# Decoder trunk on one core: M and VO stored in DRAM as high and low parts, a few multiplications and squares on ScalarE, weight sums spread anew

## The chip, the cores and the metric

One Trainium2 chip, one of its cores. The metric is the device time of one launch in microseconds, the median of several runs. The kernel before takes 3073.2 us (three runs, 3071.1 to 3073.73).

## What is computed

One inference step of a hybrid decoder trunk (one layer, width 1024) for a prompt of 2048 tokens and 8 sample tokens, all in float32. Cut to what matters here:

```
h = rmsnorm(x, g_mix);  z = h @ w_in -> u | q | k | v
group A: causal pooling of u;  group B: differential attention, 4 heads:
    w = softmax(q0 k0) - lam * softmax(q1 k1);  o = rmsnorm(w @ v, subln_g) * (1 - lam_0)
x = x + concat(pool, o) @ w_out
cross attention, 4 heads, 256 memory tokens:
    q = rmsnorm(x, g_cross) @ wq;  a = softmax(q @ mem_k / 16);  x = x + (a @ mem_v) @ wo
gated MLP with a causal convolution:  up = rmsnorm(x, g_ffn) @ w_up;  x = x + (silu(g) * a) @ w_down
y = rmsnorm(x, g_final)
```

## The kernel before

The prompt is worked through in four chunks (c = 0 to 3) of 512 tokens; the 8 sample tokens ride with chunk 3. A float32 product is made from three matmuls (`mm3`, lines 97 to 101): each operand is split into a high part in the PE's float32r format and the low rest, and high x low, high x high and low x high are added up. `split` (lines 92 to 95) makes the parts: ScalarE (ACT) casts the high part, VectorE (DVE) subtracts it.

Cross attention is folded: for each head h, M = wq_h mem_k_h^T and VO = mem_v_h wo_h are computed once (`m_head`, `vo_head`, lines 536 to 576), so that the scores of a chunk are h2 @ M and the result is A @ VO. Both are evacuated from PSUM in pieces of 128x512 by a copy on ACT (lines 557 and 573, 16 each) and stored in DRAM (`m_d`, `vo_d`) from ACT's queue; each chunk loads them again: 8 tiles of M (two for a head) in `scores`, 8 tiles of VO (one for each 128 output columns) in `vo`.

Every weight tile goes through the class `Weight` (lines 297 to 313) in three stages: 0 loads the raw tile on SyncE's queue (SP), 1 casts the high part on ACT (line 307), 2 subtracts the low part on DVE (line 310). `drive` takes the items of the program in order and calls the stages ahead of use: `look(4, 3, 2)` means that the raw load is called four tiles ahead, the cast three, the subtraction two.

```python
        if n == 0:
            self.raw = H("wraw")
            SY.dma_start(v3(self.raw, self.k), self.src)
        elif n == 1 and not self.only_raw:
            self.hi = H("whi", F32R)
            S.copy(self.hi[:, :1024], self.raw[:, :1024])
        elif n == 2 and not self.only_raw:
            self.lo = H("wlo", F32R)
            V.tensor_tensor(self.lo[:, :1024], self.raw[:, :1024], f(self.hi[:, :1024]), ALU.subtract)
```

All large tiles come from one ring of 41 buffers (`H`), the tiles of 512 columns from one ring of 6 (`St`), the small ones from a ring of 16; a new tile waits until the one that had its buffer is released. PSUM has two double banks (`PA`) and four single ones (`PB`). Each engine executes its own instructions in a fixed order, which the framework's scheduler sets from the program's items; no time in this text comes from it.

The items of the stages are woven into each other by `weave` at the end of the function: main work (PE) and extra work (norms, loads, the sample group) by their costs. Among the extras are the weight sums (`sums_items`, lines 1534 to 1573): the MLP's up-projection is done with seven products in place of eight, and needs sums of blocks of `w_up`. For each of 22 column blocks j there are two quarters q, and a quarter takes four loads of 128 KB, four DVE instructions of 256 columns (lines 1552 to 1555), one split of 128x1024 and two stores of 512 KB from POOL's queue. They are spread over four stretches of the program: the input projection of chunks 0 and 1, the attention of chunks 0 and 1, the attention of chunks 2 and 3, and the cross attention of chunks 2 and 3 right ahead of the MLP.

Other lines that the change touches: `k_evac` (line 743, a cast of the keys on DVE), `att_post1` (lines 1198 to 1211, the norm after attention: squares on ACT at 1201, their sums on DVE at 1203, the scaling on DVE at 1210), and `softmax` in `scores` (line 1306, the division of the exponentials on DVE; ACT makes the exponentials at 1304).

## Time and profile before

| what | value |
|---|---|
| median of three runs | 3073.2 us |
| the profiled execution's own time | 3072.26 us |
| its span | 3070.5 us |
| PE busy | 2934.5 us, 96% of the span |
| PE weight loads busy (beside PE) | 2644.1 us, 86% |
| DVE busy | 2243.7 us, 73% |
| ACT busy | 1353.3 us, 44% |
| POOL busy | 459.7 us, 15% |
| DMA, mean | 222 GB/s |
| mean granted PE clock | 0.982 |

The trace of this execution is read by stretch. From the start to about 115 us lie M and VO of heads 0 and 1 with the first norms; to 295 us the input projection; to 650 us the attention of chunks 0 and 1 with the projections of chunks 2 and 3; to 1057 us the attention of chunks 2 and 3, with M and VO of heads 2 and 3 and the scores of chunk 0 woven in; to 1540 us the rest of cross attention; then the MLP, with VO of chunk 3 inside its first 90 us. A matmul on this page counts as busy also while it waits in the pipeline, so the stretches are compared by idle time and by what ended it, not by the busy share.

### The profile page before, as it was taken

The page shows a single profiled execution, that of the slowest core. Times are in us where ns is not written, and L with a number is a line of the kernel's source. Part 1 is how long each engine was busy: PE and PEld are TensorE (multiplying, and loading weights), DVE is VectorE, ACT ScalarE, POOL GpSimd, SP SyncE. Part 2 cuts the span into 40 slices and gives each one's busy share as a digit, 9 for nine tenths or more (in the row PEclk, how much of TensorE's full clock was granted, in tenths as well). Part 3 has the DMA queues.
Part 4 walks back from the last instruction along what each step waited for, and adds up shares of the span by engine and source line. Part 5 has one row for each costly group of instructions (what it writes and reads, how often), then busy time and mean ns, then how long its engine had stood idle before and what let it go on. Part 6 is the DMA issues. An engine that isn't in the chain of part 4 may idle for free.

```text
span 3070.5 us, 52699 instructions
## 1 busy us (share of the span) xinstructions
PE 2934.5 (96%) x19806; PEld 2644.1 (86%) x19806; DVE 2243.7 (73%) x4168; ACT 1353.3 (44%) x2271; POOL 459.7 (15%) x865
## 2 busy tenths in 40 slices
PE   7999999999999889899999999999999999999998
PEld 6789889978888779598888899888898989899998
DVE  5745777667767577667768978888788777877777
ACT  4544455455656424343443344434444433443333
POOL 0244224200000041611100000010000010000000
PEclk9999999999999999999999999999999999999999
DMA  8797578654554467668579876777767686576762
GB/s 277 231 299 244 168 248 272 203 181 143 163 165 128 132 201 235 191 222 307 191 229 337 279 258 192 262 244 243 248 226 259 218 277 211 173 268 221 242 207 103
DMA packets 522627, 683.17 MB, mean 222 GB/s; under 512 B 29585, under 2 KB 344472, under 8 KB 522356
## 3 DMA queue, kind: packets, MB, share of 16 engines
q1 hardware_dynamic: 468637, 533.88, 53.9%
q0 software_dynamic: 39936, 135.17, 12.6%
q10 hardware_dynamic: 13798, 10.76, 1.1%
q8 instruction: 156, 2.56, 0.3%
q14 instruction: 100, 0.81, 0.1%
HBM read 549.12 MB, written 130.98 MB: 221 GB/s over the span
## 4 chain that ended last, share of the span: by engine, by line
PE 60%; DVE 6%; DMA 3%; issue 2%; ACT 2%; POOL 1%; SPq 0%; DVEq 0%; ACTq 0%; POOLq 0%
PE up L1640 15%; PE down L1756 15%; PE up L1642 7%; PE wo L487 4%; PE upB L1640 2%; PE S L99 2%; PE S L100 2%; PE S L101 2%; PE O L1175 1%; PE upB L1642 1%; PE vo L101 1%; PE vo L99 1%; PE vo L100 1%; DMA vg<-in_cache_v_dram,idx 1%; PE sc L1122 1%
## 5 line engine op out<-in xcount | busy, mean ns | idle before, releaser
L1756 PE MATMUL down<-act,whi 128*128 128x512 f32 (+1 forms) x1760 | 450.0, 350 | 0.2 <-DVE xf L1760 0.2
L1640 PE MATMUL up<-xhi,shl 128*128 128x256 f32 (+1 forms) x2816 | 405.5, 285 | 8.7 <-DVE s L1645 4.6
L1640 PEld LDWEIGHTS up<-xhi,shl 128*128 128x128 f32 x2816 | 365.5, 188 | 37.5 <-ACT s L1655 14.3
L1694 ACT ACTIVATE cc<-Uf,vec 128x512 f32<-128x512 f32 (+1 forms) x176 | 144.0, 818 | 494.7 <-DVE Uf L1645 476.9
L310 DVE TENSOR_TENSOR wlo<-wraw,whi 128x1024 fp32r<-128x1024 f32 x256 | 309.8, 1218 | 42.4 <-ACT whi L307 35.7
L1756 PEld LDWEIGHTS down<-act,whi 128*128 128x128 f32 x1760 | 285.5, 188 | 32.7 <-DVE xf L1760 1.5
L307 ACT CAST whi<-wraw 128x1024 fp32r<-128x1024 f32 x256 | 265.6, 1046 | 81.7 <-DMA wraw<-in_w_down_dram 22.6
L1756 PE MATMUL down<-act,wlo 128*128 128x512 f32 (+1 forms) x880 | 279.9, 350 | 1.9 <-DVE wlo L310 1.9
L1699 POOL COPY halo<-Uf 128x2 f32<-128x2 f32 x176 | 60.1, 342 | 1321.9 <-DVE Uf L1645 1300.2
L1642 PE MATMUL up<-xlo,shl 128*128 128x256 f32 (+1 forms) x1408 | 223.7, 281 | 0.0
L1140 ACT ACTIVATE T<-T,mn 128x1024 f32<-128x1024 f32 (+4 forms) x192 | 172.0, 897 | 103.2 <-DVE mn L1133 102.4
L1640 PE MATMUL up<-xhi,whl 128*128 128x256 f32 (+1 forms) x1408 | 199.4, 284 | 6.1 <-DVE whl L329 4.6
L1122 PE MATMUL sc<-K,Q 128*128 128x512 f32 (+5 forms) x640 | 172.5, 388 | 25.3 <-DVE mn L1133 25.1
L1640 PEld LDWEIGHTS up<-xhi,whl 128*128 128x128 f32 x1408 | 184.1, 189 | 14.6 <-DVE whl L329 5.8
L1642 PEld LDWEIGHTS up<-xlo,shl 128*128 128x128 f32 x1408 | 191.1, 188 | 0.3
L1702 DVE SCALAR_TENSOR_TENSOR cc<-Uf,vec,cc 128x512 f32<-128x512 f32 x176 | 131.5, 747 | 73.8 <-ACT cc L1694 70.2
L329 DVE TENSOR_TENSOR whl<-wraw,whl 128x512 fp32r<-128x512 f32 x264 | 178.0, 682 | 1.5 <-ACT whl L327 1.5
L1756 PEld LDWEIGHTS down<-act,wlo 128*128 128x128 f32 x880 | 153.7, 188 | 24.8 <-DVE wlo L310 3.5
L1760 DVE TENSOR_TENSOR xf<-xf,down 128x512 f32<-128x512 f32 (+1 forms) x240 | 134.8, 577 | 55.1 <-PE down L1756 53.9
L1645 DVE TENSOR_TENSOR Uf<-up,s 128x256 f32<-128x256 f32 (+1 forms) x264 | 111.4, 422 | 81.2 <-PE up L1642 78.9
L327 ACT CAST whl<-wraw 128x512 fp32r<-128x512 f32 x264 | 154.9, 615 | 30.4 <-PE up L1642 14.8
L1133 DVE CUSTOM_DVE_ANT_0 T<-sc,Dt 128x1024 f32<-128x1024 f32 (+7 forms) x128 | 125.8, 985 | 44.4 <-PE sc L1122 40.5
(434 smaller groups left out, 7068.1 us busy)
## 6 DMA issues: line engine op xcount, KB each, us to landing
shl<-s_d SPq DMA_DIRECT2D x352, 512.0 KB
wraw<-in_w_up_dram SPq DMA_DIRECT2D x264, 256.0 KB
wraw<-in_w_down_dram SPq DMA_DIRECT2D x88, 512.0 KB
ws<-in_w_up_dram SPq DMA_DIRECT2D x176, 128.0 KB
s_d<-shi POOLq DMA_DIRECT2D x44, 512.0 KB, 4.7
s_d<-slo POOLq DMA_DIRECT2D x44, 512.0 KB, 6.7
wraw<-in_w_in_dram SPq DMA_DIRECT2D x32, 512.0 KB
Q<-q_d SPq DMA_DIRECT2D x64, 256.0 KB
```

The lines of the kernel that those rows point to most:

```text
L307: S.copy(self.hi[:, :1024], self.raw[:, :1024])
L310: V.tensor_tensor(self.lo[:, :1024], self.raw[:, :1024], f(self.hi[:, :1024]), ALU.subtract)
L327: S.copy(self.hl[:, :512], self.raw)
L329: V.tensor_tensor(self.hl[:, 512:1024], self.raw, f(self.hl[:, :512]), ALU.subtract)
L1122: PE.matmul(ps[:, j * 512:j * 512 + w], v3(Q[c], 2)[:, z, self.t * P:(self.t + 1) * P], K[c][hf][:, c0:c0 + w], start=z == 0, stop=z == 1)
L1140: S.activation(tg[:, :mg], tg[:, :mg], AF.Exp, bias=mn[:, last:last + 1], scale=-1.0, accum_out=self.l[:, 2 * g + c:2 * g + c + 1])
L1640: PE.matmul(out, wi[:, k, :], xh[:, k], start=k == 0 and wi is wl, stop=False)
L1642: PE.matmul(out, wh[:, k, :], xl[:, k], start=False, stop=k == 3)
L1694: S.activation(cc[:, :w], U[:, 2:2 + w], AF.Identity, bias=vc(CB + nt), scale=vc(CWT + 2 * FT + nt))
L1702: V.scalar_tensor_tensor(cc[:, :CH], U[:, 1:1 + CH], vc(CWT + FT + nt), cc[:, :CH], ALU.mult, ALU.add)
L1756: PE.matmul(out, st["w"][0][wi][:, p, n0:n0 + P], act[:, z + c0:z + c0 + n], start=st_ and p == 0, stop=en and p == g - 1)
L1760: V.tensor_tensor(xx[:, c0:c0 + n], xx[:, c0:c0 + n], out, ALU.add)
```

## The change

M and VO are split when they are evacuated, and both parts are stored: per piece of 128x512, ACT casts the high part, DVE subtracts, and ACT's queue issues two stores. The new class `Parts` loads both parts at stage 2 and has no stages 0 and 1, so the 64 casts and 64 subtractions of these tiles go, and each tile has two loads of 512 KB. The cast of the keys goes from DVE to ACT. In `att_post1` the squares are made in four pieces that also give their sums, and the scaling is four ACT instructions. The division of the softmax is four ACT instructions of 256 columns for each head and chunk. The weight sums' blocks are spread 7, 7, 4, 4 over the four stretches; before, 5, 8, 3, 6.

```diff
-    m_d = dr.tile([NH, 2, P, 1024], F32, name="m_d")
-    vo_d = dr.tile([KT, P, 8, P], F32, name="vo_d")
+    m_d = dr.tile([NH, 2, 2, P, 1024], F32, name="m_d")
+    vo_d = dr.tile([2, KT, P, 8, P], F32, name="vo_d")
...
+    class Parts(Weight):
+        def stage(self, n):
+            if n == 2:
+                self.hi, self.lo = H("dhi", F32R), H("dlo", F32R)
+                for t, src in zip((self.hi, self.lo), self.src):
+                    SY.dma_start(f(v3(t, self.k)), src)
...
     def dram_tile(src, k):
-        return lambda: Weight(src, k)
+        return lambda: Parts(src, k)
...
+    def parts_out(ps, dst, k=1):
+        hi, lo = St("ph", F32R), St("pl", F32R)
+        split(hi[:, :512], lo[:, :512], ps)
+        for t, d in zip((hi, lo), dst):
+            S.dma_start(d, f(t[:, :512] if k == 1 else v3(t, k, 512 // k)))
...
-                ms = St("ms")
-                S.copy(ms[:, :512], ps)
-                S.dma_start(m_d[h, d2 // 2, :, (d2 % 2) * 512:(d2 % 2 + 1) * 512], ms[:, :512])
+                parts_out(ps, [m_d[h, d2 // 2, z, :, (d2 % 2) * 512:(d2 % 2 + 1) * 512] for z in range(2)])
...
-                    vs_ = St("vos")
-                    S.copy(vs_[:, :512], ps)
-                    S.dma_start(vo_d[nh * 4:(nh + 1) * 4, :, h * 2 + i, :].rearrange("n p d -> p n d"), v3(vs_, 4, P))
+                    parts_out(ps, [vo_d[z, nh * 4:(nh + 1) * 4, :, h * 2 + i, :].rearrange("n p d -> p n d")
+                                   for z in range(2)], 4)
...
-        V.tensor_copy(kh[:, :CH], kf[:, :CH])
+        S.copy(kh[:, :CH], kf[:, :CH])
...
-        S.activation(sq[:, :512], O, AF.Square)
-        ss = Tn("oss")
-        V.tensor_reduce(ss[:, 0:4].rearrange("p (a o) -> p a o", o=1), v3(sq, 4, P), AX.X, ALU.add)
+        sq, ss = St("osq"), Tn("oss")
+        for t in range(4):
+            S.activation(sq[:, t * P:(t + 1) * P], O[:, t * P:(t + 1) * P], AF.Square, accum_out=ss[:, t:t + 1])
...
-        V.tensor_tensor(v3(on, 4, P), v3(O, 4, P), bc(r, [P, 4, P], 2), ALU.mult)
+        for t in range(4):
+            S.activation(on[:, t * P:(t + 1) * P], O[:, t * P:(t + 1) * P], AF.Copy, scale=r[:, t:t + 1])
...
-                    V.tensor_tensor(e, e, bc(rc[:, :g], [P, g, 256], 2), ALU.mult)
+                    for j in range(g):
+                        S.activation(e[:, j], e[:, j], AF.Copy, scale=rc[:, j:j + 1])
...
-    order += weave(weave(half[12:24] + [item([], pool_prep)] + half[24:-8], sums_items(range(5)), 0.0, 0.6),
+    order += weave(weave(half[12:24] + [item([], pool_prep)] + half[24:-8], sums_items(range(7)), 0.0, 0.6),
...
-    order += weave(weave(late[:-16] + att23[0][:2] + late[-16:-10], att01[1]), sums_items(range(5, 13)), 0.05, 1.0) + att23[0][2:]
+    order += weave(weave(late[:-16] + att23[0][:2] + late[-16:-10], att01[1]), sums_items(range(7, 14)), 0.05, 1.0) + att23[0][2:]
...
-                   sums_items(range(13, 16)), 0.0, 0.9)
+                   sums_items(range(14, 18)), 0.0, 0.9)
...
-                   + weave(vo[2], n2[3], 0.0, 0.9) + weave(sc_[3], xop_items(0) + vo[3][:1], 0.0, 0.85), sums_items(range(16, NF)), 0.0, 0.75)
+                   + weave(vo[2], n2[3], 0.0, 0.9) + weave(sc_[3], xop_items(0) + vo[3][:1], 0.0, 0.85), sums_items(range(18, NF)), 0.0, 0.75)
```

The scheduler sets the order on the engines anew; three places matter below. The first is SP's queue in the cross attention of chunk 2, where the loads of VO (`vo_d`) for this chunk and of M (`m_d`) for chunk 3 stand among the loads of the weight sums (`ws`). Before:

```order
L304 DMA wraw<-vo_d 128x1024
L1544 DMA ws<-in_w_up_dram 128x2x128 x4
L304 DMA wraw<-vo_d 128x1024 x2
L1544 DMA ws<-in_w_up_dram 128x2x128 x4
L304 DMA wraw<-vo_d 128x1024
L1544 DMA ws<-in_w_up_dram 128x2x128 x4
L304 DMA wraw<-m_d 128x1024 x2
L1544 DMA ws<-in_w_up_dram 128x2x128 x4
L304 DMA wraw<-m_d 128x1024 x2
L1544 DMA ws<-in_w_up_dram 128x2x128 x4
L304 DMA wraw<-m_d 128x1024 x4
```

And now, from the load pair of VO's sixth tile on:

```order
L349 DMA dhi<-vo_d 128x1024
L349 DMA dlo<-vo_d 128x1024
L1556 DMA ws<-in_w_up_dram 128x2x128 x4
L349 DMA dhi<-vo_d 128x1024
L349 DMA dlo<-vo_d 128x1024
L349 DMA dhi<-vo_d 128x1024
L349 DMA dlo<-vo_d 128x1024
L349 DMA dhi<-m_d 128x1024
L349 DMA dlo<-m_d 128x1024
L1556 DMA ws<-in_w_up_dram 128x2x128 x4
L349 DMA dhi<-m_d 128x1024
L349 DMA dlo<-m_d 128x1024
```

Each tile now has two loads, and two groups of `ws` stand where there were five.

The second place is ACT's queue where M of head 3 is evacuated, inside the attention of chunks 2 and 3 (`T,l<-T,mn` are the exponentials of that attention). Before:

```order
L557 COPY ms<-M 128x512
L558 DMA m_d<-ms 128x512
L557 COPY ms<-M 128x512
L1140 ACTIVATE T,l<-T,mn 128x1024
L558 DMA m_d<-ms 128x512
L557 COPY ms<-M 128x512
L1140 ACTIVATE T,l<-T,mn 128x640
L558 DMA m_d<-ms 128x512
L557 COPY ms<-M 128x512
L307 CAST whi<-wraw 128x1024
L558 DMA m_d<-ms 128x512
```

And now:

```order
L94 CAST ph<-M 128x512
L549 DMA m_d<-ph 128x512
L549 DMA m_d<-pl 128x512
L94 CAST ph<-M 128x512
L1152 ACTIVATE T,l<-T,mn 128x1024
L549 DMA m_d<-ph 128x512
L549 DMA m_d<-pl 128x512
L94 CAST ph<-M 128x512
L1152 ACTIVATE T,l<-T,mn 128x640
L549 DMA m_d<-ph 128x512
L549 DMA m_d<-pl 128x512
```

The store of the low part (`pl`) has come into ACT's queue; it can go only when DVE has subtracted, and the exponentials and copies of attention stand behind it.

The third place is the norm after attention on ACT (`osq` squares, `rt` and `ry` the root, `om` later the transposed result), at the twelfth of its 16 occurrences. Before:

```order
L1201 ACTIVATE osq<-O 128x512
L188 ACTIVATE rt<-rv 128x4
L189 ACTIVATE ry<-rt 128x4
L1140 ACTIVATE T,l<-T,mn 128x1024
L1140 ACTIVATE T,l<-T,mn 128x384
L307 CAST whi<-wraw 128x1024
L573 COPY vos<-VO 128x512
```

And now:

```order
L1214 ACTIVATE osq,oss<-O 128x128 x4
L188 ACTIVATE rt<-rv 128x4
L189 ACTIVATE ry<-rt 128x4
L1152 ACTIVATE T,l<-T,mn 128x1024
L1152 ACTIVATE T,l<-T,mn 128x384
L307 CAST whi<-wraw 128x1024
L1222 ACTIVATE on<-O,ry 128x128 x4
L94 CAST ph<-VO 128x512
```

The scaling (`on`) was on DVE and is now on ACT, a few instructions behind the root; it waits there for five small DVE instructions that finish the root.

## Rows read from the trace of the kernel before

**Rows 1.** Busy time by stretch of the program (columns as in the heading line).
```profile
core 0: us, PE busy (x) PEld busy (x) DVE busy (x) ACT busy (x) POOL busy (x), PEclk, DMA share, GB/s
0.00:115.00 115.00, 92.07 (x564) 80.32 (x565) 68.62 (x123) 65.23 (x107) 12.46 (x55) 0.93 0.75 254
115.00:295.00 180.00, 180.00 (x1027) 155.49 (x1026) 101.16 (x165) 77.84 (x120) 81.61 (x128) 1.00 0.81 268
295.00:650.00 355.00, 333.28 (x2265) 301.87 (x2265) 253.39 (x591) 187.46 (x374) 101.45 (x159) 0.97 0.71 223
650.00:1057.00 407.00, 379.13 (x2482) 334.40 (x2482) 278.36 (x538) 231.26 (x444) 17.16 (x23) 0.97 0.45 142
1057.00:1540.00 483.00, 449.67 (x2803) 390.62 (x2803) 341.63 (x557) 181.63 (x296) 129.23 (x122) 0.96 0.68 224
```
**Rows 2.** What PE waited for, 1057 to 1540 us: us in total, times, longest.
```profile
PE vo L101 <- DVE wlo L310: 6.1, 3, 3.7
PE S L99 <- DVE wlo L310: 4.8, 3, 3.3
PE oT L1217 <- DVE on L1210: 4.2, 1, 4.2
PE R L257 <- DVE ri L207: 3.2, 1, 3.2
PE stat L250 <- DVE h2sq L232: 3.0, 1, 3.0
```
**Rows 3.** Busy time and granted clock, two stretches of 50 us in it.
```profile
1400.00:1450.00 50.00, 44.66 (x264) 38.64 (x264) 35.73 (x60) 16.71 (x17) 9.54 (x13) 0.97 0.95 333
1450.00:1500.00 50.00, 43.00 (x232) 37.41 (x231) 38.66 (x63) 18.14 (x26) 9.41 (x12) 0.90 0.67 222
```
**Rows 4.** Groups of instructions, 1057 to 1540 us: busy, mean ns, idle before.
```profile
L310 DVE TENSOR_TENSOR wlo<-wraw,whi 128x1024 fp32r<-128x1024 f32 x65 | 78.2, 1217 | 0.0
L1306 DVE TENSOR_TENSOR E<-E,rcx 128x1024 f32<-128x1024 f32 x12 | 14.7, 1227 | 0.3
L95 DVE TENSOR_TENSOR slo<-ws,shi 128x1024 fp32r<-128x1024 f32 x12 | 14.6, 1221 | 3.6 <-ACT shi L94 3.4
L307 ACT CAST whi<-wraw 128x1024 fp32r<-128x1024 f32 x63 | 64.3, 1051 | 12.9 <-DMA wraw<-vo_d 10.1 <-DMA wraw<-m_d 2.8
```
**Rows 5.** Groups by form over the whole span, VectorE.
```profile
L95 DVE TENSOR_TENSOR Alo<-AT,Ahi 128x512 fp32r<-128x512 f32 x32 | 20.7, 682 | 9.2 <-ACT Ahi L94 9.2
L1554 DVE TENSOR_TENSOR ws<-ws 128x256 f32<-128x256 f32 x44 | 18.6, 423 | 0.9
```
**Rows 6.** Groups by form over the whole span, ScalarE.
```profile
L1304 ACT ACTIVATE E<-S,nbx 128x256 f32<-128x256 f32 x64 | 29.5, 473 | 58.8 <-DVE nbx L1299 40.8 <-issue 17.6 <-DVE rt L191 0.4
L1304 ACT ACTIVATION_READ_ACCUMULATOR E<-S,nbx 128x1 f32 x64 | 13.0, 203 | 0.0
L1219 ACT ACTIVATE om<-oT,vec 128x512 f32<-128x512 f32 x16 | 11.0, 686 | 15.3 <-PE oT L1217 14.6 <-DVE plo L95 0.6
L1166 ACT COPY wT<-wT 128x128 f32<-128x128 f32 x16 | 4.2, 260 | 3.8 <-PE wT L1164 3.4 <-DMA k_d<-kh 0.3
```
**Rows 7.** Waits of PE and of ACT in the attention stretches, 295 to 1057 us.
```profile
PE sc L1122 <- DVE mn L1133: 25.1, 19, 4.2
PE O L1175 <- ACT wT L1166: 4.1, 4, 1.9
...
ACT rt L188 <- DVE rv L187: 43.4, 14, 5.0
```
**Rows 8.** Evacuations of M and VO: lines 557 and 573, 860 to 890 us; issue of M's stores.
```profile
L557 ACT COPY ms<-M x4: 577/582/587, 866.2 to 870.7; 128x512 f32<-128x512 f32 x4
L573 ACT COPY vos<-VO x4: 559/586/589, 872.9 to 881.6; 128x512 f32<-128x512 f32 x4
L558 ACTq DMA_DIRECT2D m_d<-ms x16: 325/333/367, 48.4 to 871.3; - x16
```
**Rows 9.** DMA issues: KB each, median us from issue to landing.
```profile
mix_d<-om POOLq DMA_DIRECT2D x16, 256.0 KB, 5.2
```

More of the change, by code (lines that the diff above doesn't have):

```diff
@@ L1199, in att_post1 @@
         O = att["O", qc, h]
-        sq = St("osq")
-        S.activation(sq[:, :512], O, AF.Square)
-        ss = Tn("oss")
-        V.tensor_reduce(ss[:, 0:4].rearrange("p (a o) -> p a o", o=1), v3(sq, 4, P), AX.X, ALU.add)
+        sq, ss = St("osq"), Tn("oss")
+        for t in range(4):
+            S.activation(sq[:, t * P:(t + 1) * P], O[:, t * P:(t + 1) * P], AF.Square, accum_out=ss[:, t:t + 1])
         r0 = att["rc", qc, h][:, 0:8:2]
@@ L1377, in p3_items @@
             n2 = norm(GCROSS, "h2", x1_d[c])
-        sc_ = sum([steps([dram_tile(m_d[h, 0].rearrange("p (k n) -> p k n", k=4), 4),
-                          dram_tile(m_d[h, 1].rearrange("p (k n) -> p k n", k=4), 4)], scores(h), 11.5, 4)
-                   for h in range(NH)], [])
-        vo_ = [item([], reload, 0, 16.0)] + sum([steps([dram_tile(vo_d[nt], 8)], vo(nt), 5.3, 4) for nt in range(KT)], [])
+        sc_ = sum([steps([dram_tile([m_d[h, i, z].rearrange("p (k n) -> p k n", k=4) for z in range(2)], 4)
+                          for i in range(2)], scores(h), 11.5, 4) for h in range(NH)], [])
+        vo_ = [item([], reload, 0, 16.0)] + sum([steps([dram_tile([vo_d[z, nt] for z in range(2)], 8)], vo(nt), 5.3, 4) for nt in range(KT)], [])
         vo_ += [item([], spill(x2_d))]
```

## The prediction

> **What bounds the kernel now.** I read the busy time by stretch first. In the input projection PE is busy for all of its 180 us and nothing beside it matters; in the MLP after 1540 us the change touches only its first 90 us. What can be won lies in three places: 295 to 650 us (355 us, PE busy 333.28), 650 to 1057 us (407 us, 379.13) and 1057 to 1540 us (483 us, 449.67) [rows 1]. PE idles 21.7, 27.9 and 33.3 us there, and its granted clock averages 0.97, 0.97 and 0.96: it falls from 2.4 to 1.2 GHz around the longer stops, so a stop costs more than its length.
>
> Then I read what ended PE's waits. In the last of the three, cross attention, it is mostly DVE: 6.1 us and 4.8 us on `wlo`, the low part of a weight tile, then single waits of 4.2, 3.2 and 3.0 us on norms [rows 2]. All `wlo` waits there are those of VO and M, the tiles that this change stores ready made. They come late because DVE is loaded: 78.2 us of its 341.63 are 65 such subtractions [rows 1, 4], of which 16 belong to `w_out` and 49 to M and VO (64 in all, less 8 of M for chunk 0, which stand in attention, and 7 of VO for chunk 3, in the MLP). In the attention stretches the largest wait is 25.1 us on DVE's reading of the scores, `mn`; waits on ACT are small there (4.1 us on `wT`) [rows 7].
>
> **The change part by part.** Durations are those of the profiled execution, 3072.3 us, 0.9 us below the median of 3073.2.
>
> *Cross attention, 1057 to 1540 us.* DVE loses 49 x 1.217 = 59.6 us, the 12 softmax divisions of 1.227 = 14.7 us, and the weight sums of two blocks: four quarters, each 4 x 0.423 + 1.221 = 2.91, together 11.7 us [rows 4, 5]. That is 86 of 341.63 us. ACT loses 49 x 1.051 = 51.5 us of casts and about 4 us of `shi`, and gets 48 x 0.473 = 22.7 us of divisions [rows 4, 6]. What PE gets back:
> - the `wlo` waits: 6.1 + 4.8 = 10.9 us [rows 2];
> - the wait on `h2sq` in the same crowded 100 us, 3.0 us [rows 2];
> - the clock lost there: 50 x 0.03 + 50 x 0.10 = 6.5 us [rows 3];
> - half of the 4.2 and 3.2 us on `on` and on the root, where DVE's queue is only a part of the chain: 3.7 us.
>
> Together 24.1 us. Against it stand the loads. Before, a raw tile was asked for four tiles ahead; both parts are now asked for two ahead, in SP's order, and nothing but the ring of 41 buffers holds SP back. A pair is 1 MB where it was 0.5 MB: 49 x 0.52 = 26 MB more, and four quarters less (0.5 MB read, 1 MB written each, 6 MB). 483 us at 224 GB/s are 108 MB [rows 1]; 128 MB would be 265 GB/s, below the 333 GB/s at a DMA share of 0.95 that one stretch reaches [rows 3]. The new wait lies between nothing and 10.9 us (every `wlo` wait comes back as a wait for a load); I take 4, nearer to nothing, since a tile that needs no cast and subtraction after landing is also ready sooner. Sum for this stretch: -20 us.
>
> *Attention, 295 to 1057 us.* DVE loses for each of 15 norms a sum and a scaling of 512 columns, 2 x 0.682 = 1.36 us [rows 5], 20.5 us; one block of weight sums leaves the first part and one comes into the second; 8 `wlo` (9.7 us) and 8 half-size divisions (5.5 us) go, 16 subtractions of 0.682 for M and VO come (10.9 us). Net -25 of 531 us, 5%, with the key casts uncounted. ACT gets for each norm 4 x (0.260 + 0.203) for squares with sums, less the 0.58 of one piece of 512 columns, and 4 x (0.260 + 0.10) for the scaling, the 0.10 being what a scale vector adds (0.686 against 0.582): 2.7 us, 15 times, 41 us; 16 divisions come and 8 casts go, about even [rows 4, 6, 8]. Net +40 of 419 us, 10%. 5% of the 25.1 us on DVE is a gain of 1.3 us, 10% of the 4.1 us on ACT a loss of 0.4 [rows 7]. I take 0; the bounds are -20 (half of the 25.1 and a third of the clock loss, 762 x 0.03 = 23 us, go) and +15 (below, among the rivals).
>
> ScalarE does more slowly here what VectorE did: four divisions take 4 x 0.473 = 1.89 us, where DVE took 1.227 [rows 4, 6]. The Trainium skill (ScalarE: Activation LUTs, Rules for kernel authors) says that multiplications belong on VectorE; its figures (What ACT_TABLE_LOAD costs: about 280 ns + 0.833 ns per column with a pointer operand) would make a piece an estimated 493 ns, 4% above the row. By that rule the move would cost and not give. By the rows, all divisions together are 64 x 0.473 = 30.3 us on ACT for 12 x 1.227 + 8 x 0.682 = 20.2 us on DVE, 10 us more of engine time, and I count that as nothing while ACT is the emptier engine (181.63 against 341.63 us) [rows 1].
>
> *Storing M and VO, before 115 us and 740 to 882 us.* 32 pieces: DVE +0.682 each, ACT's queue one more issue of 0.333 [rows 5, 8], and a PSUM bank is held until DVE is done. The cast replaces the copy at the same length. Nothing is taken away, so a gain is excluded; if every piece were exposed it would be 32 x 1.015 = 32.5 us. PE has other work woven in here, so I take a quarter, +8 us, for the reason given at the last rival.
>
> *Weight sums.* Two blocks more in the input projection are four quarters, 11.7 us of DVE in a stretch where it is busy 101.16 of 180 us and PE for all of it [rows 1]: 0. If that cover were gone, at most the 11.7 us. The seven tiles of VO inside the MLP are changed in the same way; I take 0, inside the bounds of the load waits above.
>
> Sum: -20 + 0 + 8 = -12 us, 3060 for the profiled execution, **3061 us** for the median.
>
> **The rivals.**
> - *More than that.* DVE's relief reaches the attention stretches: -20 there and no new load waits (-4): 3061 - 24 = 3037. For it speaks that 25.1 us end on one DVE instruction; against it, that DVE is relieved there by only 5%.
> - *Loads late.* In VO of chunk 2, at 333 GB/s, and in M of chunk 3 each pair lands late, so that 10.9 us of waits and 6.5 us of clock stay: 17.4 less the 4 counted, 3061 + 13 = 3074, no change. For it speak the short lead and the DMA share of 0.95 [rows 3]; against it, that two groups of `ws` stand where five stood.
> - *ACT blocked in attention.* ACT already stands 43.4 us, 14 times, at `rt` for DVE [rows 7], 3.1 us each time. `on` is a second such stop, 15 x 3.1 = 46 us, and exponentials and `wT` are behind it. If a third reaches PE: +15, 3076, no change. This is where the rule named above would show. Against it: ACT idles 45% of these stretches.
> - *Slower: the ring of six small buffers fills up.* A piece now takes two of its buffers and holds them through cast, subtraction and store: 0.58 + 0.68 + 5.2 (a store of the same 256 KB) = 6.5 us [rows 5, 8, 9]. Heads' pieces come eight in 866.2 to 881.6 us and the last copy, 16 us [rows 8]: 16 x 6.5 / 16 = 6.5 buffers of 6, and attention's `wT` copies need the same ring. ACT's queue, which issues the stores, stands meanwhile for DVE. It decides when a store takes over 6 - 1.3 = 4.7 us. Then all 32.5 us are paid, not 8: 3061 + 24 = 3085. Against it: only two of four heads come as densely, and PE's order is made anew.
>
> **How the numbers follow.** The forecast (3047 to 3067) gets 0.52, the larger gain 0.13, late loads 0.08, ACT blocked 0.09, the full ring 0.18. About 0.2%, 6.1 us, is what a measurement of this kernel can tell from no change. Faster is 0.52 + 0.13 = 0.65, the same 0.08 + 0.09 = 0.17, slower 0.18. The range goes from the larger gain, 3036, to the full ring, 3086; some 0.16 is left outside.
>
> **What would show it.** After the change there is no wait on `wlo` in `vo` and `S`; waits on loads of `dhi` or `dlo` there would sum to about 4 us (over 10: late loads). The granted clock between 1400 and 1500 us is near 1.00. DVE is busy some 86 us less after 1057 us. In attention the waits on `mn` stay near 25 us, those on `wT` near 4 (over 12: ACT blocked). Waits of PE, or of ACT at `ph` and `wT`, that end on a store of `pl` or `ph`, would show the ring. The forecast is wrong if the time from 1057 us to the MLP shrinks by under 10 us, or if the time to that point grows by over 15.

## The result: 29 us slower, and the profile after

The changed kernel takes 3102.8 us (median of four runs) against 3073.5 us for the kernel before on the same chip: a ratio of 1.0100, 95% interval 1.0082 to 1.0117. One of the four runs, 4770.4 us at a granted clock of 0.555, is a slow one, and the ratios in this text are of fast runs alone, so that they lie up to 0.0008 from the quotients of the medians. Forecast were 3061 us. The profiled execution has a span of 3102.1 us, 31.6 us longer.

Where the time went is read by comparing the start of the same matmul in both traces. The shift is 17.1 us when the input projection is under way (119 us before), 26.2 at attention's first scores (295), 43.5 at the first output projection (649), 51.0 at the first VO (1084) and still at VO of chunk 2 (1418), but 31.3 at the MLP (1532) and 31.9 at the end. So 51 us are lost before cross attention, and 20 of them come back in the last 113 us ahead of the MLP.

Busy time of the changed kernel in the same stretches, moved by these shifts (answers to [rows 1]; the columns are PE, PE's weight loads, DVE, ACT, POOL, granted clock, DMA share, GB/s):

```profile
0.00:132.00 132.00, 98.44 (x564) 85.75 (x565) 78.50 (x139) 65.14 (x107) 12.51 (x54) 0.87 0.74 247
132.00:321.00 189.00, 182.29 (x1026) 156.49 (x1024) 107.99 (x176) 86.18 (x133) 87.99 (x136) 0.99 0.87 292
321.00:693.00 372.00, 341.90 (x2272) 307.80 (x2271) 237.08 (x559) 205.06 (x483) 97.07 (x155) 0.95 0.66 206
693.00:1108.00 415.00, 380.00 (x2478) 333.00 (x2477) 269.90 (x530) 239.61 (x516) 20.75 (x27) 0.97 0.52 167
1108.00:1571.00 463.00, 440.26 (x2803) 384.90 (x2801) 261.47 (x475) 154.22 (x304) 117.51 (x114) 0.97 0.79 276
```

The reader is to see two things. Cross attention is 463 us long where it was 483, with 80 us less of DVE (261.47 against 341.63), as forecast. And the input projection, in which PE was busy for all of its time, now has 6.7 us of idle PE; the stretch ahead of it has a clock of 0.87 where it was 0.93.

What PE waited for in cross attention, answering to [rows 2]:

```profile
PE R L257 <- DVE ri L207: 11.2, 1, 11.2
PE sao L1028 <- ACT vh L94: 5.8, 3, 3.5
PE oT L1229 <- ACT on L1222: 2.2, 1, 2.2
PE sao L1028 <- DVE vl L95: 2.2, 4, 0.6
```

And two stretches of 50 us at its end, answering to [rows 3]:

```profile
1450.00:1500.00 50.00, 50.00 (x302) 44.20 (x301) 30.60 (x60) 9.62 (x12) 9.16 (x14) 1.00 1.01 372
1500.00:1550.00 50.00, 50.00 (x359) 47.02 (x358) 32.13 (x54) 22.87 (x51) 5.05 (x6) 1.00 0.88 330
```

The two waits on `sao`, the sample group's attention, stand in the list of the kernel before as well, with 6.6 and 2.6 us; the first is the longest there, though [rows 2] do not have it. No wait on `wlo` is left and none on `dhi` or `dlo`; PE is busy without a gap at full clock while the transfers run at 372 GB/s. Most of what was forecast for this stretch is there. The wait on `ri` is not: half of its 3.2 us was to go, and it is 11.2 us. What brought the gain is another question.

### The profile page after: what moved, and what is told of

The parts are those of the page before. It is cut to its first block, busy times and chain, and to the rows that moved or that the text cites. A ratio compares the mean times of both kernels' runs of the same rounds, so it can differ in the third digit from the quotient of the medians.

```text
span 3102.1 us, 52923 instructions
## 1 busy us (share of the span) xinstructions
PE 2943.7 (95%) x19806; PEld 2649.8 (85%) x19806; DVE 2148.2 (69%) x4068; ACT 1353.6 (44%) x2463; POOL 459.0 (15%) x865
## 3 DMA queue, kind: packets, MB, share of 16 engines
q0 software_dynamic: 39936, 135.17, 12.3%
## 4 chain that ended last, share of the span: by engine, by line
PE 61%; DVE 4%; issue 3%; DMA 2%; ACT 1%; POOL 1%; DVEq 0%; SPq 0%; ACTq 0%; POOLq 0%
PE up L1652 15%; PE down L1768 15%; PE up L1654 7%; PE wo L496 4%; PE upB L1652 2%; PE S L99 2%; PE S L100 2%; PE S L101 2%; PE vo L99 2%; PE vo L101 2%; PE vo L100 1%; PE upB L1654 1%; PE O L1187 1%; DMA vg<-in_cache_v_dram,idx 1%; PE sc L1134 1%
## 5 line engine op out<-in xcount | busy, mean ns | idle before, releaser
L310 DVE TENSOR_TENSOR wlo<-wraw,whi 128x1024 fp32r<-128x1024 f32 x192 | 232.8, 1219 | 32.1 <-ACT whi L307 28.1
L307 ACT CAST whi<-wraw 128x1024 fp32r<-128x1024 f32 x192 | 200.2, 1045 | 69.8 <-DMA wraw<-in_w_down_dram 23.6
L1134 PE MATMUL sc<-K,Q 128*128 128x512 f32 (+5 forms) x640 | 174.4, 391 | 30.9 <-DVE mn L1145 23.9
L1652 PEld LDWEIGHTS up<-xhi,whl 128*128 128x128 f32 x1408 | 184.5, 189 | 14.4 <-DVE whl L329 5.8
L496 PE MATMUL z<-h1hi,wlo 128*128 128x512 f32 (+1 forms) x480 | 160.5, 367 | 3.7 <-ACT xT L670 3.7
```

The source lines that it names most:

```text
L496: PE.matmul(out, w[wi][:, kt, :], kslice(z, kt, c0, n), start=i == 0, stop=i == 3 * KT - 1)
L1134: PE.matmul(ps[:, j * 512:j * 512 + w], v3(Q[c], 2)[:, z, self.t * P:(self.t + 1) * P], K[c][hf][:, c0:c0 + w], start=z == 0, stop=z == 1)
L1652: PE.matmul(out, wi[:, k, :], xh[:, k], start=k == 0 and wi is wl, stop=False)
```

## The experiments

The change has three parts that can be made alone: the **parts** of M and VO (P), the work moved to **ScalarE** (A) and the **sums** spread anew (S). Two more questions came up on the way: what fills the stretch before 130 us, and where the sums stand best. The table has every run: how many us the shift against the kernel before grew in each stretch (named by the times of before, from the profiled executions), the sum of that, and the time of all runs as a ratio to the kernel before on the same chip. The sums come from single executions and the traces from more than one chip, so they stand up to 6 us from what the ratio says, 12 and 16 in e8 and e7; a step is read where it is larger than that or returns in several kernels.

| kernel | 0-119 | -295 | -649 | -1084 | -1418 | -1532 | -end | sum | median us | ratio (95%) |
|---|---|---|---|---|---|---|---|---|---|---|
| changed (P, A, S) | 17.1 | 9.1 | 17.3 | 7.5 | -0.1 | -19.6 | 0.6 | 31.9 | 3102.8 | 1.0100 (1.0082-1.0117) |
| e1: P, A | 19.3 | 0.1 | 12.8 | -0.6 | 3.3 | -9.3 | -1.3 | 24.3 | 3091.6 | 1.0061 (1.0043-1.0079) |
| e2: S | -0.5 | 8.3 | 4.5 | 4.9 | -0.9 | -16.7 | -0.1 | -0.4 | 3070.4 | 0.9996 (0.9985-1.0007) |
| e3: A, S | 1.4 | 15.3 | 13.2 | 6.1 | -1.6 | -16.7 | 0.4 | 18.2 | 3090.9 | 1.0063 (1.0046-1.0080) |
| e4: P, S | 17.3 | 8.9 | 5.0 | 18.5 | 0.8 | -16.1 | -0.1 | 34.3 | 3105.8 | 1.0107 (1.0091-1.0124) |
| e5: P | 18.0 | 0.0 | -0.1 | 3.9 | 14.4 | -9.2 | 0.7 | 27.7 | 3099.3 | 1.0071 (1.0054-1.0088) |
| e6: changed, lambda later | 9.3 | 16.2 | 11.2 | 8.3 | 5.4 | -18.4 | -0.4 | 31.6 | 3107.9 | 1.0108 (1.0092-1.0125) |
| e7: changed, pl from POOL | 11.6 | 16.7 | 13.1 | 12.3 | 14.6 | -19.0 | 1.9 | 51.2 | 3112.7 | 1.0116 (1.0099-1.0133) |
| e8: changed, ring of 8 | 14.3 | 12.2 | 13.4 | 20.6 | 20.9 | -17.8 | 0.8 | 64.4 | 3130.9 | 1.0171 (1.0154-1.0188) |
| e9: before, 2 blocks in MLP | -1.5 | 0.4 | 0.2 | 0.2 | -2.6 | -16.5 | 6.1 | -13.8 | 3059.6 | 0.9963 (0.9950-0.9975) |
| e10: A | 0.4 | 0.7 | 8.1 | -4.1 | 1.7 | -0.8 | 0.4 | 6.5 | 3078.6 | 1.0023 (1.0013-1.0034) |
| e11: P, A, 2 blocks in MLP | 18.3 | 0.1 | 11.4 | -2.4 | -1.0 | -19.1 | 4.1 | 11.3 | 3085.5 | 1.0043 (1.0026-1.0060) |
| e12: the same, lambda later | 7.7 | 1.8 | 11.2 | -0.5 | -1.6 | -19.5 | 8.9 | 8.0 | 3081.1 | 1.0028 (1.0016-1.0040) |
| e13: before, 32 subtractions | 6.6 | 1.1 | 3.0 | 6.3 | -4.1 | -2.1 | -0.9 | 10.0 | 3085.3 | 1.0044 (1.0029-1.0059) |
| e14: before, 2 blocks, later | 0.1 | 0.1 | -0.1 | 0.4 | -3.2 | -15.0 | 1.3 | -16.6 | 3055.3 | 0.9948 (0.9934-0.9961) |
| e15: before, 3 blocks in MLP | 1.6 | 0.0 | 2.6 | 1.2 | -3.7 | -18.0 | 7.9 | -8.5 | 3060.1 | 0.9965 (0.9951-0.9978) |

### One part undone or done alone (e1 to e5, e10)

**e1.** The sums spread as before.

```diff
-sums_items(range(7)) ... range(7, 14) ... range(14, 18) ... range(18, NF)
+sums_items(range(5)) ... range(5, 13) ... range(13, 16) ... range(16, NF)
```

> The changed kernel (3102.8) with the weight sums spread 5, 8, 3, 6 as before; all else as changed. Theory A (the two blocks added to the input projection stretch make its loads and casts late): the some 9 us that were lost between 115 and 295 us come back, and cross attention gets back two blocks (four more quarters on VectorE): about 3096. Theory B (storing M and VO in parts) and theory C (the work moved to ScalarE): 3103 or up to 10 more, since cross attention is fuller again. By all theories the 17 us lost before 130 us stay under B and C.

The 9 us of the input projection came back whole, so they are the sums'. Half of the gain ahead of the MLP went (-19.6 to -9.3), so at least half of that was the sums' too; from 1084 us on, 6.0 us are left of 19.7.

**e2.** The kernel before with this respreading alone (the opposite diff).

> The kernel before (3073.5) with the weight sums spread 7, 7, 4, 4, nothing else changed. Theory A: slower by some 9 us in the input projection, won back in part in cross attention, which loses 11.7 us of VectorE work: 3073 to 3082. Theories B and C: no loss before 295 us, and a gain in cross attention: 3063 to 3073.

It gains 16.7 us in the 113 us ahead of the MLP, by two blocks of sums fewer and nothing else; the changed kernel gains 19.6 there. It gives back 8.3 us in the input projection and 9.4 in attention. Its waits of PE, 180 to 300 us, and then of ACT, 190 to 235 us, show the first of these:

```profile
PE z L487 <- ACT xT L658: 3.0, 1, 3.0
PE xTp L654 <- ACT ks L754: 1.6, 1, 1.6
...
ACT shi L94 <- DVE ws L1555: 5.3, 3, 2.7
ACT kf L742 <- DMA k_d<-kh: 4.5, 1, 4.5
```

and its busy time there (columns as above):

```profile
200.00:220.00 20.00, 19.55 (x92) 15.65 (x91) 9.11 (x16) 7.42 (x10) 9.69 (x15) 1.00 1.03 391
220.00:240.00 20.00, 14.94 (x77) 11.74 (x76) 8.47 (x15) 13.43 (x26) 11.52 (x20) 0.91 0.92 285
```

The transfers are at 391 GB/s. Between 150 and 250 us a store of the keys' high part lands after 5.5 us (14 stores), where before it took 3.3 us (16 stores):

```profile
k_d<-kh POOLq DMA_DIRECT2D x14, 128.0 KB, 5.5
```

```profile
k_d<-kh POOLq DMA_DIRECT2D x16, 128.0 KB, 3.3
```

The first line is of this kernel, the second of the kernel before. The small buffers are held longer, ACT's copy `kf` stands 4.5 us for one, the copies of x (`xT`) behind it on ACT come late, and PE stands. The cast `shi` of a sum waits for DVE's addition, 5.3 us in three stops; in the last of them, 1.8 us, DVE itself had stood 4.4 us for that `kf`. The forecast had looked at DVE's cover there; the transfers were what had none.

**e3.** M and VO stored and loaded as before in the changed kernel, that is A and S together.

```diff
-                parts_out(ps, [m_d[h, d2 // 2, z, ...] for z in range(2)])
+                ms = St("ms")
+                S.copy(ms[:, :512], ps)
+                S.dma_start(m_d[h, d2 // 2, ...], ms[:, :512])
...
-        return lambda: Parts(src, k)
+        return lambda: Weight(src, k)
```

> The changed kernel with M and VO stored and loaded as before (copy, one store, cast and subtraction at each load); squares, scaling, keys and division stay on ScalarE, sums stay 7, 7, 4, 4. Theory B (storing in parts): the 17 us before 130 us and the 10 us between 740 and 900 us come back, and the gain of 20 us in cross attention goes: about 3096, with the first score matmul of attention some 17 us earlier than in the changed kernel. Theories A and C: nothing comes back before 295 us, so 3103 plus some 15 to 20, about 3120.

The 17 us before 119 us are the parts': 1.4 are left. The gain ahead of the MLP is 16.7 us without the parts, 19.6 with them. But A, which costs nothing that shows beside P, costs 20 us beside S alone (3090.9 against 3070.4); the input projection loses 15.3 us. ACT stands there 9.2 us for buffers that late stores of the keys hold (5.3 at `kf`, 3.9 at `ks`), where e2 has 4.5. That it is the keys' cast, now on ACT, which adds to this is likely and not shown: A was not taken apart.

**e4.** Squares' sums, scaling, keys' cast and division on VectorE again.

```diff
-            S.activation(sq[:, t * P:(t + 1) * P], O[...], AF.Square, accum_out=ss[:, t:t + 1])
+        S.activation(sq[:, :512], O, AF.Square)
+        V.tensor_reduce(ss[:, 0:4]..., v3(sq, 4, P), AX.X, ALU.add)
...
-                        S.activation(e[:, j], e[:, j], AF.Copy, scale=rc[:, j:j + 1])
+                    V.tensor_tensor(e, e, bc(rc[:, :g], [P, g, 256], 2), ALU.mult)
```

> The changed kernel with squares' sums, scaling, cast of the keys and division of the exponentials on VectorE again; M and VO in parts and sums 7, 7, 4, 4 stay. Theory C (ScalarE's added work): the some 10 to 14 us lost between 295 and 1085 us come back: 3089 to 3093. Theories A and B: 3103, within 5 either way; the 26 us lost before 295 us stay by all.

Theory C misses: nothing comes back on the whole (1.0107 against 1.0100). Attention's first half is 12 us shorter without A, its second half 11 us longer.

**e10.** A alone, the opposite diff on the kernel before.

> The kernel before with only the work moved to ScalarE (squares with sums, scaling, cast of the keys, division of the exponentials). With parts it cost nothing or won 2 us (3102.8 against 3105.8; 3091.6 against 3099.3), with the respread sums alone it cost 18 us (3090.9 against 3070.4). Theory C1 (it costs only where the small buffers are held by late stores of the keys, that is with the two extra blocks in the input projection): 3066 to 3076 here, nothing lost before 300 us. Theory C2 (it blocks ScalarE in attention, the forecast's rival, and cross attention's relief hides it): 3080 to 3092, lost between 295 and 1085 us.

The time lies between the two theories, 2.6 us above what C1 allowed and 1.4 below C2. The place is C2's: nothing is lost before 295 us, 8 us between 295 and 649, and half of that returns by 1084. The new instructions (the changed kernel's, by form over the whole span) are

```profile
L1319 ACT ACTIVATE E<-E,rcx 128x256 f32<-128x256 f32 x64 | 28.0, 504 | 9.3 <-DVE rcx L1317 9.2
L1222 ACT ACTIVATE on<-O,ry 128x128 f32<-128x128 f32 x64 | 18.1, 364 | 11.6 <-DVE ry L1219 11.0 <-DVE rcu L1164 0.6
L1214 ACT ACTIVATE osq<-O 128x128 f32<-128x128 f32 x64 | 16.7, 272 | 6.1 <-PE O L1187 6.1
L1214 ACT ACTIVATION_READ_ACCUMULATOR osq<-O 128x1 f32 x64 | 13.1, 204 | 0.0
```

A piece of the division takes 504 ns, where 473 were assumed from [rows 6]. The estimate of 493 from the Trainium skill (ScalarE: Activation LUTs, What ACT_TABLE_LOAD costs) was 2% from it. The rule of the Trainium skill that multiplications belong on VectorE (ScalarE: Activation LUTs, Rules for kernel authors) has the sign of A alone, 1.0023; beside P, A shows no loss, and no run shows a gain from A that is clear of its interval (1.0061 against 1.0071, 1.0100 against 1.0107).

**e5.** The parts alone, on the kernel before (the diff of e3 the other way).

> The kernel before with only M and VO stored and loaded in parts; sums 5, 8, 3, 6 and ScalarE's work as before. In the runs so far the parts cost 17 us before 130 us, whatever stands beside them, and the respread sums cost 8 us in the input projection and give 15 to 18 us in cross attention. Theory B (parts cost where they are stored, and win little where they are loaded, because the sums were what filled cross attention): +17 by 130 us, some 4 to 8 more by 900 us, 5 to 9 back in cross attention: 3085 to 3095. Rival (the parts win the 20 us forecast in cross attention, and other work gives it back): +17, then -20: 3068 to 3076.

This is the run that answers the forecast's main term. The parts cost 18 us before 119 us, and win nothing in cross attention: +14.4 between 1084 and 1418 us, -9.2 after that, 5 us lost in all. DVE is busy 379.9 us from 930 to 1560 us there, where it was 444.8 before, and yet PE gets nothing back. In the last 113 us, with six blocks of sums beside them, the doubled loads are late by 7.8 us, which is the place of the forecast's second rival (PE's waits, 1080 to 1600 us; the first line stands before 1418 us):

```profile
PE R L257 <- DVE ri L207: 9.4, 1, 9.4
...
PE vo L99 <- DMA dhi<-vo_d: 6.4, 1, 6.4
...
PE vo L101 <- DMA dlo<-vo_d: 1.4, 1, 1.4
```

In the changed kernel, with four blocks, these two waits on loads are gone. The wait on `ri`, 3.2 us before [rows 2], is 7 to 12 us in every kernel with parts, but also 6.5 and 7.1 us in e3 and e10, which have A and no parts. It is a norm whose small DVE instructions stand between products of the sample group (`kg`), for which DVE waits until the gathered keys have landed (the changed kernel's DVE in order of time; in brackets the idle time before an instruction):

```profile
1169.64 0.15 DVE L207 SCALAR_TENSOR_TENSOR ri<-rt,ri 128x4 f32<-128x4 f32 x1
1172.83 1.23 DVE L944 TENSOR_TENSOR kg<-kg,qb 128x1024 f32<-128x1024 f32 x1 [3.04 <-DMA kg<-in_cache_k_dram,idx]
1173.98 0.16 DVE L205 SCALAR_TENSOR_TENSOR rt<-ri,rv 128x4 f32<-128x4 f32 x1
```

### The stretch before 130 us (e6 to e8, e13)

PE's waits in the changed kernel, 40 to 132 us:

```profile
PE wqT L559 <- DVE wqlo L95: 7.2, 1, 7.2
PE pool L99 <- DVE plo L95: 4.3, 1, 4.3
PE VO L99 <- DVE pl L95: 3.1, 1, 3.1
```

The same list of the kernel before, 40 to 115 us, has 4.4 and 0.9 us on the first two and nothing on the third. That is 9.3 us more; the granted clock between 60 and 100 us averages 0.74 where it was 0.95 and 0.88, another 20 x 0.21 + 20 x 0.14 = 7.0 us. Together 16.3 of the 17.1; the other waits on both lists sum to the same 6.5 us. What makes `wqlo` late stands in DVE's order of time:

```profile
77.86 1.22 DVE L310 TENSOR_TENSOR wlo<-wraw,whi 128x1024 fp32r<-128x1024 f32 x1
86.02 0.29 DVE L146 TENSOR_TENSOR lp<-lq 128x128 f32<-128x128 f32 x1 [6.94 <-DMA lq<-in_lam_k_dram]
...
87.47 2.36 DVE L310 TENSOR_TENSOR wlo<-wraw,whi 128x1024 fp32r<-128x1024 f32 x2
89.74 1.88 DVE L95 TENSOR_TENSOR wqlo<-wqT,wqhi 128x512 fp32r<-128x512 f32 x3
```

DVE stands 6.9 us for lambda's small loads, which nothing needs here. They are issued on ACT's queue; in the kernel before that was at 67.1 to 69.2 us and they had landed when DVE came to them, now it is 10 us later (the first two lines below). ACT's queue had stood for DVE at the stores of `pl` (the last two): these two issues wait for subtractions that end at 69.1 and 70.3 us, and the cast behind them starts after 3.6 idle us. How much of the 10 us such stands are, e7 tells.

```profile
L143 ACTq DMA_DIRECT2D lq<-in_lam_q_dram x2: 443/488/533, 77.8 to 78.9; - x2
L143 ACTq DMA_DIRECT2D lq<-in_lam_k_dram x2: 442/452/462, 78.4 to 79.4; - x2
69.08 1.62 ACTq L549 DMA_DIRECT2D vo_d<-pl  x2
70.75 1.05 ACT L307 CAST whi<-wraw 128x1024 fp32r<-128x1024 f32 x1 [3.59 <-DMA vo_d<-ph]
```

**e6.** Lambda formed later, in the input projection.

```diff
-    ... [item([], pool_load), item([], lambda_)] + n1[1][1], 0.2, 1.0)
+    ... [item([], pool_load)] + n1[1][1], 0.2, 1.0)
...
-    ... half[12:24] + [item([], pool_prep)] + half[24:-8] ...
+    ... half[12:24] + [item([], pool_prep), item([], lambda_)] + half[24:-8] ...
```

> The changed kernel (3102.8) with the item that loads and forms lambda moved from the projection of M's and VO's second head into the input projection, where nothing needs it early. Theory B1 (of the 17 us, the larger part is that VectorE stands 6.9 us at lambda's product for loads that ScalarE's queue now issues 10 us later, since it stood for the stores of pl): M of head 1 starts some 7 us earlier and the clock around it stays up, in all 8 to 12 us less before 130 us: 3091 to 3095. Rival B2 (it is the load on VectorE and the held PSUM banks; lambda only stands where the time would be lost anyway): under 3 us.

The wait of `wqT` on `wqlo` goes and the loss to 119 us falls from 17.1 to 9.3 us: B1 for this part. The end is no earlier: the input projection loses 16.2 in place of 9.1. It has the seven blocks of sums, and its transfers are at the limit:

```profile
180.00:220.00 40.00, 40.00 (x179) 32.39 (x178) 23.86 (x39) 15.44 (x21) 20.62 (x30) 1.00 1.04 369
220.00:260.00 40.00, 30.90 (x144) 24.74 (x143) 14.05 (x23) 20.69 (x38) 18.95 (x30) 0.87 0.86 281
```

What was saved ahead of a full stretch was only waited for in it.

**e7.** The stores of `pl` from POOL's queue.

```diff
-        for t, d in zip((hi, lo), dst):
-            S.dma_start(d, f(t...
+        for q, t, d in zip((S, G), (hi, lo), dst):
+            q.dma_start(d, f(t...
```

> The changed kernel with the 32 stores of the low parts issued from POOL's queue in place of ScalarE's; nothing else. Theory B1 (ScalarE's queue stands for VectorE at each pl store, and what is behind comes late): lambda's loads come as early as before, 10 to 15 of the 17 us come back, and some at 740 to 930 us too: 3085 to 3093. Rival B2 (VectorE's 32 subtractions and the banks that they hold): under 4 us. Rival B3 (the ring of six small buffers): none or slower, since POOL issues later than ScalarE.

5.5 us less to 119 us, so the stand of ACT's queue is a part, and some half of what B1 expected. Lambda's loads, with no store of `pl` ahead of them on ACT's queue, are issued 4 us earlier than in the changed kernel and still 6 us later than before, and DVE still stands for them:

```profile
L143 ACTq DMA_DIRECT2D lq<-in_lam_q_dram x2: 352/677/1002, 73.4 to 74.3; - x2
81.70 0.29 DVE L146 TENSOR_TENSOR lp<-lq 128x128 f32<-128x128 f32 x1 [4.45 <-DMA lq<-in_lam_k_dram]
```

The 5.5 us are lost again by 295, as in e6. Beyond, this kernel is slower than the changed one, mostly between 1084 and 1418 us (14.6), where no such store stands; why was not settled. Its profiled execution is 11 us above its median, so part of that may be this one execution.

**e8.** Eight small buffers, 40 large ones.

```diff
-NBUF_H = 41
+NBUF_H = 40
...
-    sp = ctx.enter_context(tc.tile_pool(name="sp", bufs=6))
+    sp = ctx.enter_context(tc.tile_pool(name="sp", bufs=8))
```

> The changed kernel with eight small buffers in place of six, and 40 large ones in place of 41. Theory B3, which is the forecast's rival (the ring of six is full of ph and pl, and of kf, kh, kl and ks whose stores land later in the input projection): waits that end on stores of vo_d, m_d and k_d go, 8 to 15 us of the 17 and some of the 9 us at 240 us come back: 3080 to 3092. Rival B1 and B2 (order of ScalarE's queue, VectorE): under 4 us, 3099 to 3106.

Only 2.8 us come back to 119 us, and to 295 the loss is the same 26 us: the full ring, the forecast's last rival, is a small part of it at most, though its price came nearest to the result. In the changed kernel's own trace the waits of ACT that are put down to a store of `ph` or `pl`, the sign that the forecast named, are 3.6, 2.4 and 2.1 us, and the 3.6 are the stand for DVE shown above. The kernel of e8 is 22 us slower than the changed one by the ratios; both sizes changed, so the loss from 649 to 1418 us can't be put on the one or the other.

**e13.** The kernel before with the subtraction alone (its result is not read); here for M, and the same for VO. It takes one small buffer more for each piece, for as long as the subtraction lasts.

```diff
                 S.copy(ms[:, :512], ps)
+                V.tensor_tensor(St("pl")[:, :512], ps, ms[:, :512], ALU.subtract)
```

> The kernel before with the 32 subtractions of M and VO made when they are evacuated (VectorE, from the PSUM bank, into a small buffer that nothing reads), but M and VO stored once and loaded as before. Parts alone cost 18 us by 130 us, of which moving lambda took away 8 to 9. Theory B2 (the rest is VectorE: 16 x 0.68 us more before 130 us and the banks held until then): about 9 us lost by 130 us, lambda's product not late: 3080 to 3087. Theory B1 (all of it is ScalarE's queue, which stands for VectorE at the stores of pl): under 3 us by 130 us, 3071 to 3077.

6.6 us to 119 us, between the two theories but nearer to VectorE: PE waits for the bank that DVE still reads, and for `wqlo` as before:

```profile
PE wqT L544 <- DVE wqlo L95: 3.9, 1, 3.9
PE VO L99 <- DVE pl L575: 3.5, 1, 3.5
...
PE pool L99 <- DVE plo L95: 1.9, 1, 1.9
```

Lambda's loads are issued at 74.1 to 75.9 us here, as late as in e7 and without any store of `pl`, and DVE stands 1.6 us for them. So the subtractions alone, with the banks that they hold and the new order on ACT that comes with them, already put these loads 6 us back; the stores of `pl` add the other 4. The shares of the some 17 us therefore overlap: the subtractions alone cost 7 (e13), taking lambda away gives back 8 to 11 (e6, e12), taking the stores of `pl` off ACT's queue 5.5 (e7). With lambda away what is left, 8 to 9 us, is near to what the subtractions cost alone.

### Where the sums stand best (e9, e11, e12, e14, e15)

**e9.** The kernel before, with the last two blocks in the MLP's first pass. No part of the change is in it.

```diff
-... sums_items(range(16, NF)), 0.0, 0.75)
+... sums_items(range(16, 20)), 0.0, 0.75)
...
-    order += weave(ffn_items(0, xops[0], vo[3][1:]), sc_items + n3[1], 0.15, 0.9)
+    order += weave(weave(ffn_items(0, xops[0], vo[3][1:]), sums_items(range(20, NF)), 0.25, 0.7),
+                   sc_items + n3[1], 0.15, 0.9)
```

> The kernel before with the sums spread 5, 8, 3, 4 and the last two blocks in the MLP's first pass, where they are needed last. Theory A2 (of the respreading, the two blocks that left cross attention gave 17 us, and the blocks that entered elsewhere took it back: 8 us in the input projection, 4 to 6 each in attention): the loss stays away and the gain comes, 10 to 17 us less: 3057 to 3066. Rival (the MLP's first pass is as full, or any new order costs some 6 us at 560 us): 3068 to 3075.

Faster by 0.37%. Little moves before 1084 us (0.7 us), and from there to the MLP it wins 19.1 us, 16.5 of them in the last stretch: what the changed kernel won there (19.7 and 19.6) is had without any of its other edits. The two stretches of [rows 3] in this kernel:

```profile
1400.00:1450.00 50.00, 49.14 (x281) 42.54 (x280) 36.13 (x62) 17.86 (x20) 8.32 (x12) 1.00 0.87 310
1450.00:1500.00 50.00, 48.48 (x359) 45.87 (x357) 42.29 (x61) 25.93 (x52) 4.99 (x6) 1.00 0.56 192
```

DVE is no less busy than before (36.13 and 42.29 us, where it was 35.73 and 38.66), PE 4.5 and 5.5 us busier and at full clock. Of the waits on `wlo` of [rows 2] the 6.1 us in `vo` are gone, of the 4.8 in `S` there are left

```profile
PE S L99 <- DVE wlo L310: 3.3, 3, 1.8
```

So DVE's total load was not what held PE; what stood at the wrong moment were the sums. One of those waits on `wlo`, followed back in the kernel before, shows how:

```profile
1479.55 0.69 DVE L1352 TENSOR_TENSOR x<-x,vo 128x512 f32<-128x512 f32 x1 [2.51 <-PE vo L101]
1480.15 0.42 DVE L1555 TENSOR_TENSOR ws<-ws 128x256 f32<-128x256 f32 x1
1480.61 1.04 ACT L94 CAST shi<-ws 128x1024 fp32r<-128x1024 f32 x1 [7.71 <-DVE ws L1555]
1481.56 2.94 ACT L307 CAST whi<-wraw 128x1024 fp32r<-128x1024 f32 x3
1481.68 1.22 DVE L95 TENSOR_TENSOR slo<-ws,shi 128x1024 fp32r<-128x1024 f32 x1 [1.11 <-ACT shi L94]
1484.19 0.50 PE L99 MATMUL S<-wlo,h2hi 128*128 128x256 f32 x1 [3.27 <-DVE wlo L310]
```

DVE's last addition of a sum stands behind an instruction that waits for PE. ACT waits 7.7 us for it at `shi`, with the casts of weight tiles (`whi`) behind, and DVE goes on to the next `wlo`, at 1482.8 us, only after the sum's own split (`slo`). PE waits 3.3 us for that `wlo`. So a part of what a block costs there is its place in two queues; how much its loads and stores add no run tells.

**e11.** The changed kernel with the sums as in e9.

> The changed kernel with the sums spread 5, 8, 3, 4 and two blocks in the MLP. If the shares add up as the runs so far say (17 us before 130 us for storing in parts; 9 us in the input projection and some 6 at 990 to 1030 us for the two blocks there and the one in late attention; cross attention relieved as in the changed kernel): 3102.8 - 9 - 6 = 3088, between 3082 and 3094. If the loss of the input projection is not the sums' but the parts' or ScalarE's, 3098 to 3104.

3085.5, in the middle of what the shares give: the input projection loses nothing, the stretch ahead of the MLP gains 19.1. With e9 as the base, P and A together cost some 25 us (1.0043 against 0.9963).

**e12.** The same with lambda later, as in e6.

> The kernel of the run before this one with lambda's loads also moved later. With seven blocks in the input projection the 8 us that lambda's move saved before 130 us were lost again by 260 us. If that is because the transfers bound that stretch there, they stay saved here, where it has five blocks: 8 us less than the run before, some 3080. If the saving is lost for another reason (the norms of chunks 2 and 3 come no earlier), it is within 3 us of the run before.

Of the 10.6 us saved by 119 us, 8.1 are still there at the MLP's start (e11 is 7.2 us late there, this kernel 0.9 early): what bound e6 was the full input projection. Inside the MLP 4.8 are lost, and 4.4 are left in the medians (1.0028 against 1.0043, with intervals that overlap). The MLP's loss was not followed up.

**e14 and e15.** As e9, with the two blocks between 45% and 80% of the pass, and with three blocks between 40% and 75%.

```diff
-    ... sums_items(range(20, NF)), 0.25, 0.7) ...
+    ... sums_items(range(20, NF)), 0.45, 0.8) ...
```

> The kernel before with the last two blocks of weight sums in the MLP's first pass as in the run that came to 3059.6, but between 45% and 80% of it in place of 25% to 70%. There cross attention won 20 us and the MLP gave back 6, 3 of them between 1600 and 1780 us, where VO of chunk 3 and the transfers (share 0.9) still stand. If that is the reason, 3 us come back: 3055 to 3058. If it is VectorE's work as such, it stays at 3058 to 3062.

> The same with three blocks in the MLP's first pass, between 40% and 75%. If cross attention is still short of VectorE and transfers with four blocks, a fifth of what the first two gave comes once more: 3050 to 3056. If PE waits there for nothing that the sums hold up any more, the same or up to 4 us more than with two blocks: 3056 to 3063.

e14 has the lowest time of these kernels: 3055.3 us against 3070.6, 0.52% less than before, with 1.3 us given back in the MLP in place of e9's 6.1; its interval overlaps that of e9. A third block moved wins 3 us more ahead of the MLP and gives back 7.9 in it: no gain over two.

## Why the prediction was wrong

The forecast was 42 us too low and the time lies outside the range (3036 to 3086), on the side to which 0.18 had been given. The time to cross attention grew by 51 us, where the text called itself wrong from 15 on. By its own terms:

- **Cross attention, -20.** Measured -19.7 from 1084 us to the MLP. The size was right and the cause wrong, so the size was luck. The sum had put the relief on all 86 us of VectorE work alike, and only 11.7 of these were the weight sums'. Alone, the sums win 17.6 us there (e2), and 14 to 21 in every pair of kernels that differ by them alone. The parts lose 5 alone (e5) and 2 beside S (e4 against e2), and win 7 beside A (e1 against e10) and 1 beside both (the changed kernel against e3): no effect of one sign. A alone loses 1 (e10). With two blocks moved elsewhere there is a gain of 19 with DVE as loaded as before (e9). The waits on `wlo` ended on DVE, but 7.6 of their 10.9 us went with the sums, while the casts and subtractions stayed (e2, e9). And the wait on `ri`, of which half was to go, grew by 8 us.
- **Storing M and VO, +8, "a quarter".** This is the step that failed most plainly. Measured 17 to 18 us for the heads 0 and 1 alone and some 4 for 2 and 3 (e5, 649 to 1084), 22 of the 32.5 that the text had as its upper bound. PE's other work did not cover it. The ring, named as the way to get there, was not it (e8). Two things that a piece does besides its 1.015 us are named in the text and have no price in the sum: a bank is held until DVE is done, which with the subtraction costs 7 us (e13), and ACT's queue stands for DVE, 5.5 us (e7). Both make unrelated loads behind them (lambda) late, which stop DVE in turn (e6).
- **Weight sums in the input projection, 0.** Measured 8 to 9 us (e1, e2). The step argued from DVE, busy 101 of 180 us, and PE's full 180 us; it did not look at the transfers, whose share of 0.81 stands in the same row [rows 1]. Inside the bound of 11.7 us that it gave, for another reason.
- **Attention, 0, bounds -20 to +15.** Measured 24.8 us from 295 to 1084 us, beyond the bound; some 4 of it belongs to storing. DVE's `mn` waits stayed as said (23.9 us for 25.1 of [rows 7]); those on `wT` went from 4.1 to 7.5 us, those on ACT's `U` (the copy of u) from 3.8 to 7.4, and a new one came, 6.4 on DVE's `oss` (the norm's sums of squares). At 364 to 366 us `on`, a copy of pool and `wT` stand ahead of `U` on ACT, as the third rival had it, here. The granted clock of the first half fell from 0.97 to 0.95, an estimated 372 x 0.02 = 7 us. Alone, A loses 4 us there, P 4 and S 9, together 17; the other 8 belong to no part alone. A and S together give 19, 6 more than apart; what meets there was not settled.
- **The rivals.** The loads late came in part in e1 and e5, with waits of 7.7 and 7.8 us where the text had set 10 as the sign, and the changed kernel escaped them through its four blocks. The one that ended slower had the right place and the right sign: it lets storing cost 32.5 us, and 22 were measured. Of its two mechanisms the ring was the wrong one, and the stand of ACT's queue for DVE, which it names beside the ring, a part of the right one.

## What to carry to other kernels

A gain read from a crowded stretch belongs to the whole crowd: before it is put on the edit at hand, ask which of the instructions standing there can be moved away alone, and try that first. An operation that waits for another engine is priced with everything behind it in its own queue, loads for unrelated work above all. And a stretch in which the compute engine is always busy has no free room in it if its transfers are at their limit; what is saved ahead of it is lost again there.

## What the runs showed of the hardware

The transfers of one core reached 391 GB/s over 20 us (e2) and 372 over 50 us in the changed kernel (385 in e11), where the stretch in [rows 3] showed 333; PE was busy without a gap beside the 372. A store of 128 KB landed after 5.5 us where it took 3.3, with a mean over that 100 us of 335 GB/s in place of 302: 11% more rate went with two thirds more latency. With a scale taken from a column of a tile, a piece of 256 columns took 504 ns on ScalarE and one of 128 columns 364 ns; a copy of 128 columns without one (`wT`) took 283 ns in the same trace.
